# Later turns of q and k, pairs of output blocks, and stored weight pairs in a two-layer encoder kernel

## The chip, the cores and the metric

One Trainium2 chip, one of its cores. The metric is the device time of one execution in microseconds (us), as the median of several runs. The engines are named as the profile names them: PE (TensorE matmul), PEld (its weight load, which overlaps PE), DVE (VectorE), ACT (ScalarE), POOL (GpSimd) and SP (SyncE, which here issues most DMAs; ACT issues a few). A name such as L475 is a line of the kernel before the change.

## The reference

The input x is 2048 tokens by 1024 channels. Two layers run over it:

```
# layer 0: pooling mixer
h = rms_norm(x, a_norm);  u, z = split(h @ w_in)
pooled = trailing means of u over 2, 4, 8, 16 tokens (one window per group of 256 channels) - u
x = x + ((pooled @ w_group) * scale * silu(z)) @ w_out
x = x + (p[0] @ ple_w[0]) * sigmoid(x @ ple_gate_w[0])
# shared keys and values, once
k, v = split(rms_norm(x, kv_norm) @ w_kv);  k = rms_norm per head of 64 (16 heads)
# layer 1: stick-breaking attention
q, z = split(rms_norm(x, b_norm) @ b_w_in);  q = rms_norm per head
a[t, s] = beta[t, s] * product over s < j < t of (1 - beta[t, j]),  beta = sigmoid(q k / 8),  s < t only
x = x + ((a @ v) * silu(z)) @ b_w_out
x = x + (p[1] @ ple_w[1]) * sigmoid(x @ ple_gate_w[1])
```

Everything is float32. The kernel reaches that precision by splitting each operand into a high and a low part (a "pair") and adding three matmuls: high by high, high by low, low by high.

## The kernel before

**Tiles and chunks.** The tokens are cut into four chunks of 512 (`NSUB`, index s or c). Activations are tiles of 128 channels by 512 tokens, kept as pairs. For each chunk `first_part(s)` runs the mixer (`mixer`), its output projection (`out_steps`), the gated embedding (`gate_steps`), the gate z of layer 1 (`gate_z`), and q, k and v of heads 0 to 7 (`kvq(s, kind, 0)`); `second_part(s)` runs q, k and v of heads 8 to 15. `post(c)` is layer 1's projection and embedding (again `out_steps` and `gate_steps`). These generators yield after every matmul and are joined in one stream.

**Attention beside it.** The attention loop at the end of the kernel goes over slots (query chunk c, head h, key chunk kc), 160 of them with four steps each. Step n does `front` (logits by two matmuls L628 and L629, a sigmoid, a scan L635 on DVE), `turn` of the step `LAG_T` = 5 before (four transposes L646, then the pair: ACT copy L649 and DVE subtraction L650, into an `at` tile, two buffers) and `gather` of the step `LAG_G` = 6 before (two matmuls L658 and L659 with v). Between these, `fill` takes matmuls from the stream, at a rate per step that depends on the chunk: 26.8 in the first, 6.2 in the last (`rate`). So the dense work hides attention's chains. `post(3)` runs alone at the end. Everything before the q, k, v of the first chunk's heads 8 to 15 also runs without attention.

**Accumulators.** `dense()` takes PSUM banks: from six when nothing but the stream runs (`solo`), from two, named psd, beside attention. `turned()` takes one of the two psa banks, which the attention turns use too.

**Weights.** `plan` lists all weight units in the order of use: [128 channels, 2 (high and low), 512 values], 512 KB as a pair, 256 KB raw. `unit` loads one on SP (L146), through an `io` buffer (six of them), and splits it on ACT (L135, L129) and on DVE or POOL (L136, L131); if the unit is marked `keep`, the pair is stored to DRAM (L150), and later uses load the pair itself (L143). There are nine buffers for pairs (`UNITS`); `give_back` frees one after its last matmul and `pump` starts the next. In a block of two outputs (`product`) the four units go back one after another during the second output. In `kvq` all eight units of a product stay until its fourth token tile (j = 3) and go back one by one there. Weights of z and of the layer 0 gate z are kept; q, k and v weights (`plan_wide`) are split again in each chunk: 48 units a chunk.

**q and k.** `kvq` makes token-major tiles of 128 tokens by 512 channels, 24 matmuls each (L421). `keyed` scales them (ACT L459), squares them (ACT L461), sums per head (DVE L463), takes the power -1/2 on POOL (L113, L114) and scales the rows (DVE L466). After the fourth tile it appends four closures `finish(m)` to the list `lag`: four transposes on PE (L475), the pair on ACT and DVE (L481 and L482, or L117 and L118), a store (L484). `kvq` of the next kind calls them after matmul groups kt = 2 and kt = 5 of its token tiles j = 0 and j = 1. `valued` shifts v by one token through DMAs on ACT's queue (L437 to L444) and writes the last row of each tile to `ve`; `differences` makes the pair and stores it.

**Other steps that the change touches.** `load_ends` reads `ve` back for the attention of a group of heads, turns it by four tiny transposes (L614) and an ACT copy (L616). `gate_z` computes the norm of its input after its first output and needs the broadcast of it (`token_norm`, `bcast`, L266, L274) to evacuate that output. `fold(g)` multiplies the group map into the u weights at the start (L248); `prep(s)` loads and splits a chunk of x.

**Order.** Each engine works through its own queue in a fixed order, SP's and ACT's DMA issues included. The order is made when the program is built: as written, but a planner with costs of its own may put an instruction that it holds ready ahead of one that waits.

## Time and profile before

| What | us |
|---|---|
| median of 3 runs | 2962.69 |
| lowest and highest | 2959.23, 2965.87 |
| the profiled execution | 2961.81 |
| its span, first to last instruction | 2960.0 |
| PE busy | 2763.0 |
| DVE busy | 1955.7 |
| ACT busy | 1355.7 |
| POOL busy | 966.2 |

The mean clock granted to PE over the span is 0.975. The DMAs moved 588.96 MB, 199 GB/s on average. Busy time of PE is made of modelled ends: matmuls overlap, so a busy PE can still run below its pace, but an idle PE is idle. A row of waits reads: the engine and the tile and line that waited, `<-` what ended the wait, then total us, number of waits, the longest. In a table of stages a row has the stretch, its length, the busy us of PE, PEld, DVE, ACT and POOL with their instruction counts, the granted clock, the DMA share and GB/s. In a list in order of time a row has its start, its length, the engine and line, the operation with out<-in, the count merged, and in brackets the idle time before it.

### The profile page before, as it was taken

Reading aid. Unit: us, or ns where it says so; the run is one execution under the profiler, and the core shown is the slowest. Engines: PE = TensorE matmul, PEld = TensorE weight load, DVE = VectorE, ACT = ScalarE, POOL = GpSimd, SP = SyncE. Lnnn points to the kernel's source line nnn. Section 1 sums busy time; section 2 is a strip of 40 time slices with the busy share of each in tenths; the row PEclk is TensorE's granted clock in tenths of the full one; section 3 lists DMA queues with packets and bytes.
Section 4 is the critical chain, followed back from the end, with each engine's and each line's share of the span. In section 5 each row is a group of like instructions: output and inputs, shape, how many; then the busy total and the mean of one; then the engine's idle time right before and its main releaser. Section 6 shows DMA issues by size and latency. Waiting matters only on the chain. (4 is left out here: it accounts for less than half of the span.)

```text
span 2960.0 us, 39525 instructions
## 1 busy us (share of the span) xinstructions
PE 2763.0 (93%) x13376; PEld 2260.2 (76%) x13376; DVE 1955.7 (66%) x2513; ACT 1355.7 (46%) x2642; POOL 966.2 (33%) x961
## 2 busy tenths in 40 slices
PE   6999898999888999998899999999899999999989
PEld 5878677777776787876777877877678888888767
DVE  6645454655455677756667878776767877778862
ACT  4334453344544344545543455455544444444541
POOL 3454433555533244443222445222211211111111
PEclk9999999999989999999999999999999999999999
DMA  8747468877755755654556445745466777657534
GB/s 282 262 135 252 160 216 293 263 230 260 230 172 185 249 165 153 196 178 144 176 193 213 154 146 153 250 139 163 154 202 206 241 218 226 214 192 228 181 122 164
DMA packets 279062, 588.96 MB, mean 199 GB/s; under 512 B 33830, under 2 KB 66598, under 8 KB 278860
## 3 DMA queue, kind: packets, MB, share of 16 engines
q1 hardware_dynamic: 272096, 577.96, 60.8%
q10 hardware_dynamic: 6764, 8.47, 1.1%
q8 instruction: 107, 1.75, 0.3%
q14 instruction: 95, 0.78, 0.1%
HBM read 442.07 MB, written 135.86 MB: 195 GB/s over the span
## 5 line engine op out<-in xcount | busy, mean ns | idle before, releaser
L635 DVE TENSOR_TENSOR_SCAN pp<-pp,zeros 128x512 f32<-128x512 f32 (+3 forms) x640 | 779.2, 1219 | 119.5 <-POOL pp L633 91.4
L421 PE MATMUL psd<-wpair,x 128*128 128x512 f32 x2304 | 623.9, 408 | 2.2 <-DVE wpair L136 1.4
L649 ACT CAST at<-psa 128x512 fp32r<-128x512 f32 (+3 forms) x640 | 332.8, 520 | 606.0 <-PE psa L646 526.5
L650 DVE TENSOR_TENSOR at<-psa,at 128x512 fp32r<-128x512 f32 (+3 forms) x640 | 384.9, 603 | 320.1 <-ACT at L649 318.2
L421 PEld LDWEIGHTS psd<-wpair,x 128*128 128x128 f32 x2304 | 437.0, 196 | 89.7 <-DVE wpair L136 4.1
L646 PE MATMUL psa<-ident,pp 128*128 128x128 f32 x2176 | 348.9, 275 | 12.9 <-DVE at L650 6.4
L646 PEld LDWEIGHTS psa<-ident,pp 128*128 128x128 f32 x2176 | 278.4, 142 | 94.4 <-DVE pp L635 8.3
L631 ACT ACTIVATE pp<-psl 128x512 f32<-128x512 f32 (+3 forms) x640 | 343.6, 538 | 10.2 <-PE psl L629 7.2
L221 PE MATMUL psd<-x,wpair 128*128 128x512 f32 x768 | 304.7, 397 | 9.7 <-ACT sg L397 6.1
L223 PE MATMUL psd<-x,wpair 128*128 128x512 f32 x768 | 303.7, 395 | 0.2 <-DVE x L118 0.2
L226 PE MATMUL psd<-x,wpair 128*128 128x512 f32 x768 | 302.9, 394 | 0.0
L628 PE MATMUL psl<-kk,qa 128*128 128x512 f32 (+3 forms) x640 | 285.1, 446 | 0.0
L633 POOL TENSOR_SCALAR_AFFINE_SELECT pp<-pp 128x128 f32<-128x128 f32 x256 | 89.5, 350 | 554.4 <-ACT pp L631 553.8
L659 PE MATMUL pso<-at,vv 128*128 128x512 f32 (+3 forms) x640 | 239.9, 375 | 20.8 <-DVE at L650 20.3
L658 PE MATMUL pso<-at,vv 128*128 128x512 f32 (+3 forms) x640 | 233.9, 366 | 5.8 <-ACT at L649 5.7
L629 PE MATMUL psl<-kk,qb 128*128 128x512 f32 (+3 forms) x640 | 236.4, 369 | 0.0
L221 PE MATMUL psd<-xp,wpair 128*128 128x512 f32 x512 | 202.2, 395 | 6.2 <-DMA wpair<-once 3.8
L223 PE MATMUL psd<-xp,wpair 128*128 128x512 f32 x512 | 201.7, 394 | 0.0
L226 PE MATMUL psd<-xp,wpair 128*128 128x512 f32 x512 | 201.5, 393 | 0.0
L136 DVE SCALAR_TENSOR_TENSOR wpair<-wraw,gains,wpair 128x512 fp32r<-128x512 f32 (+1 forms) x224 | 165.9, 782 | 35.0 <-ACT wpair L135 34.5
L221 PEld LDWEIGHTS psd<-x,wpair 128*128 128x128 f32 x768 | 145.7, 190 | 40.4 <-ACT sg L397 7.5
L135 ACT ACTIVATE wpair<-wraw,gains 128x512 fp32r<-128x512 f32 (+1 forms) x224 | 145.7, 688 | 57.4 <-DMA wraw<-in_w_kv_dram 16.9
(134 smaller groups left out, 4664.8 us busy)
## 6 DMA issues: line engine op xcount, KB each, us to landing
wpair<-once SPq DMA_DIRECT2D x240, 512.0 KB
kk<-kd SPq DMA_DIRECT2D x320, 128.0 KB
vv<-vd SPq DMA_DIRECT2D x160, 256.0 KB
wpair<-wf SPq DMA_DIRECT2D x64, 512.0 KB
wraw<-in_w_kv_dram SPq DMA_DIRECT2D x128, 256.0 KB
once<-kp SPq DMA_DIRECT2D x36, 512.0 KB
once<-wpair SPq DMA_DIRECT2D x32, 512.0 KB
wraw<-in_a_w_out_dram SPq DMA_DIRECT2D x64, 256.0 KB
```

The costliest lines, as they stand in the source:

```text
L221: T.matmul(ps, hi, acts[kt][:, 0], start=(i == 0), stop=False)
L223: T.matmul(ps, hi, acts[kt][:, 1], start=False, stop=False)
L226: T.matmul(ps, lo, acts[kt][:, 0], start=False, stop=(i == n))
L421: T.matmul(ps, ck["x2"][kt][:, xh, tk], u[:, wh, 0], start=(kt == 0 and xh == wh), stop=(kt == KT - 1 and wh == 1))
L628: T.matmul(ps[:, :w], qa[:, qs], kk[:, :w], start=True, stop=False)
L629: T.matmul(ps[:, :w], qb[:, qs], kk[:, :w], start=False, stop=True)
L631: A.activation(out=pp[:, r0:], in_=ps[:, :w], func=AF.Sigmoid, scale=-1.0)
L635: V.tensor_tensor_scan(out=pp[:, r0:][:, ::-1], data0=pp[:, r0:][:, ::-1], data1=zeros.to_broadcast([P, w]), initial=1.0 if st["diag"] els ...
L646: T.transpose(pt[:, j * P : (j + 1) * P], pp[:, r0 + kt * P : r0 + (kt + 1) * P], ident)
L649: A.copy(out=at[:, 0, cs], in_=pt[:, cs])
L650: V.tensor_tensor(out=at[:, 1, cs], in0=pt[:, cs], in1=f(at[:, 0, cs]), op=ALU.subtract)
L659: T.matmul(po[:, cs], vv[:, kt, :], at[:, 1, cs], start=False, stop=(st["last"] and kt == 3))
```

## The change

Eight edits:

- `LAG_G` goes from 6 to 7, the `at` tile gets a third buffer, an `io` buffer is taken away (five), and a slot's v is loaded at its neighbour's step 3 instead of 2.
- The four `finish` calls move from (j, kt) = (0, 2), (0, 5), (1, 2), (1, 5) to (1, 2), (1, 5), (2, 1), (2, 4). `vs` moves from the `row` buffers, which hold q's or k's rows longer now, to `tmp`.
- `product2` takes the first two outputs of `out_steps`, `gate_steps` and `gate_z` together: the first three units for both outputs, then the last unit for both; all units go back at its end.
- `gate_z` copies its first two outputs out of PSUM unscaled, computes the norm after them, and puts the broadcast into the next block.
- q, k, v weights are kept: the first chunk stores the pairs, the others load them.
- `load_ends` reads the ends by four DMAs on ACT's queue, in transposed order, 4 bytes an element, with no transposes.
- At the start `fold` requests the u tiles (on SP) before it takes the group map's weights; these weights and half of the first chunk's x are requested on ACT's queue, and only two weight units may be out until half of the first chunk of x is split.
- The first chunk's x is loaded ahead (`load_first`) into q, k, v and pp buffers.

```
-LAG_T, LAG_G = 5, 6
+LAG_T, LAG_G = 5, 7
-    io = flat("io", 6)
+    io = flat("io", 5)
-    att = ... tag="at", name=nm, bufs=2)
+    att = ... tag="at", name=nm, bufs=3)
...
-        nc.sync.dma_start(out=raw, in_=src[:, kts[0] : kts[-1] + 1])
+        wq["by"].dma_start(out=raw, in_=src[:, kts[0] : kts[-1] + 1])
...
-        while wq["out"] < len(plan) and wq["out"] - wq["back"] < UNITS:
+        while wq["out"] < len(plan) and wq["out"] - wq["back"] < wq["cap"]:
...
-            plan.append(((nm, b, kt), src[b], (kt,), W5, gain, False))
+            plan.append(((nm, b, kt), src[b], (kt,), W5, gain, True))
...
+    def product2(pss, us, acts):
+        n = sum(len(kts) for _, kts in us)
+        i = [0, 0]
+        for part, back in ((us[:-1], False), (us[-1:], True)):
+            for k in range(2):
+                for u, kts in part:
+                    for e, kt in enumerate(kts):
+                        hi, lo = (u[:, l, e, k * P : k * P + P] for l in range(2))
+                        T.matmul(pss[k], hi, acts[kt][:, 0], start=(i[k] == 0), stop=False)
+                        yield
+                        T.matmul(pss[k], hi, acts[kt][:, 1], start=False, stop=False)
+                        yield
+                        i[k] += 1
+                        T.matmul(pss[k], lo, acts[kt][:, 0], start=False, stop=(i[k] == n))
+                        yield
+        for _ in us:
+            give_back()
...
+    def load_first():
+        for o in range(KT):
+            xin = (qryt, ppt, keyt, valt)[(0, 2, 0, 3, 0, 2, 0, 3)[o]]("xin", F32)
+            (nc.sync, nc.scalar)[o % 2].dma_start(out=xin, in_=x[o * P : (o + 1) * P, 0:W5])
+            first_x.append(xin)
...
@@ out_steps, gate_steps
+            pss = [dense(), dense()] if b == 0 else []
+            if pss:
+                yield from product2(pss, us, acts)
...
-                if kt in (2, 5) and j < 2 and lag:
+                if lag and (j, kt) in ((1, 2), (1, 5), (2, 1), (2, 4)):
                     lag.pop(0)()
...
-        vs = row("vs")
+        vs = tmp("vs")
...
@@ gate_z
+        yield from product2(pss, us, ck["x2"])
+        for k in range(2):
+            zr = row("zr")
+            A.copy(out=zr, in_=pss[k])
+            first.append(zr)
+        ck["r2"] = token_norm(ck["acc2"], "y")
...
+                for i, _ in enumerate(product(ps, us, ck["x2"], k * P, k)):
+                    if o == 2 and i == 20:
+                        ck["rb2"] = rb = bcast(ck["r2"], "y")
...
@@ load_ends
-        for m in range(4):
-            T.transpose(pt[:, 0, 4 * m : 4 * m + 4], raw[0:4, m * P : (m + 1) * P], ident[0:4, 0:4])
+        for j in range(4):
+            nc.scalar.dma_start(out=en[:, :, j], in_=ve[c][b][j].rearrange("(m q) -> q m", q=P))
...
+    start = fold(3)
+    next(start)
+    load_first()
...
-            if j == 2 and i + 1 < len(slots):
+            if j == 3 and i + 1 < len(slots):
                 begin_v(i + 1)
```

More of the change, by code (lines that the diff above doesn't have):

```diff
@@ L123, in trunk_kernel @@
     plan = []
-    wq = {"out": 0, "taken": 0, "back": 0}
+    wq = {"out": 0, "back": 0, "cap": 2, "by": nc.scalar}
     held = deque()
@@ L295, in prep @@
         for o in range(KT):
[L296 to L297 removed]
+            if s:
+                xin = io("xin")
+                nc.sync.dma_start(out=xin, in_=x[o * P : (o + 1) * P, s * W5 : (s + 1) * W5])
+            else:
+                xin = first_x[o]
             pr = pair("xp")
@@ L368, in out_steps @@
                 nc.sync.dma_start(out=xr, in_=residual(2 * b + k))
-                ps = dense()
-                yield from product(ps, us, acts, k * P, k)
+                if pss:
+                    ps = pss[k]
+                else:
+                    ps = dense()
+                    yield from product(ps, us, acts, k * P, k)
                 V.tensor_tensor(out=xr, in0=ps, in1=xr, op=ALU.add)
@@ L389, in gate_steps @@
             us, ul = take(4), take(1)
+            pss = [dense(), dense()] if b == 0 else []
+            if pss:
+                yield from product2(pss, us, x1)
             for k in range(2):
@@ L393, in gate_steps @@
                 G.tensor_tensor(out=xj, in0=f(x1[o][:, 0]), in1=f(x1[o][:, 1]), op=ALU.add)
-                ps = dense()
-                yield from product(ps, us, x1, k * P, k)
+                if pss:
+                    ps = pss[k]
+                else:
+                    ps = dense()
+                    yield from product(ps, us, x1, k * P, k)
                 sg = tmp("sg")
@@ L511, in gate_z, with put @@
         ck = chunk[s]
-        for b in range(4):
+        def put(o, zr):
+            sg = tmp("sg")
+            A.activation(out=sg, in_=zr, func=AF.Sigmoid)
+            G.tensor_tensor(out=zr, in0=zr, in1=sg, op=ALU.mult)
+            nc.sync.dma_start(out=zd[s][o], in_=zr)
+        us = take(4)
+        pss = [dense(), dense()]
+        yield from product2(pss, us, ck["x2"])
+        first = []
+        for k in range(2):
[3 more added lines that the diff above has]
+        ck["r2"] = token_norm(ck["acc2"], "y")
+        for b in range(1, 4):
             us = take(4)
@@ L713, in trunk_kernel @@
                            op0=ALU.mult, op1=ALU.mult)
-    for _ in fold(3):
+    wq["by"] = nc.sync
+    for _ in start:
         pass
     side = prep(0)
-    for _ in range(KT):
+    for _ in range(4):
         next(side)
-    for _ in fold(2):
+    wq["cap"] = UNITS
+    second = fold(2)
+    next(second)
+    for _ in range(4):
+        next(side)
+    for _ in second:
         pass
```

40 lines of the change are left out of this document (20 added, 20 removed).

## The prediction

> **What bounds the kernel now.** I read the page's head, then the waits of TensorE (PE), then a table of stages, then the instructions around one wait.
>
> ```profile
> span 2960.0 us, 39525 instructions
> PE 2763.0 (93%) x13376; PEld 2260.2 (76%) x13376; DVE 1955.7 (66%) x2513; ACT 1355.7 (46%) x2642; POOL 966.2 (33%) x961
> ```
>
> PE is busy 93% of the span and nothing else comes near it, so a gain must come out of PE's 197 us of idle time (2960.0 - 2763.0) or out of time at half clock. Who ends PE's waits, in us in total, times, longest:
>
> ```profile
> PE pst L475 <- DVE qs L466: 70.8, 16, 9.7
> PE psd L248 <- ACT uh L239: 24.4, 4, 19.3
> PE pso L659 <- DVE at L650: 20.3, 29, 2.7
> PE psd L221 <- ACT mp L117: 9.8, 4, 4.7
> ...
> PE psd L221 <- DVE zr L312: 6.0, 3, 3.6
> ...
> PE pso L658 <- ACT at L649: 5.7, 6, 2.4
> ...
> PE psd L223 <- POOL mp L118: 4.7, 5, 1.7
> PE pst L266 <- POOL r L114: 4.0, 4, 1.5
> ...
> PE pst L614 <- DMA ends<-ve: 3.7, 2, 2.9
> ```
>
> By line, with the idle time before each group behind the bar:
>
> ```profile
> L475 PE MATMUL pst<-ident,qs 128*128 128x128 f32 x256 | 47.1, 300 | 83.5 <-DVE qs L466 70.8 <-DVE at L650 5.9 <-ACT op L117 5.4
> ```
>
> The turns of q and k (L475) own 83.5 us of idle time. The matmuls of q, k and v:
>
> ```profile
> L421 PE MATMUL psd<-wpair,x 128*128 128x512 f32 x2304 | 623.9, 408 | 2.2 <-DVE wpair L136 1.4 <-ACT wpair L135 0.6
> ```
>
> They wait 2.2 us in all: weights are never late today. By stage (start, the four q, k, v stages, the end of attention), with the granted clock, the DMA share and GB/s in the last columns; the last row is a stretch in which the DMAs are full:
>
> ```profile
> 0.00:41.00 41.00, 17.68 (x104) 17.05 (x105) 24.62 (x74) 22.20 (x44) 14.61 (x17) 0.92 0.80 277
> 295.00:474.00 179.00, 155.48 (x701) 126.09 (x700) 80.87 (x116) 81.29 (x140) 64.64 (x65) 0.94 0.61 198
> 778.00:981.00 203.00, 175.97 (x833) 143.19 (x832) 108.50 (x154) 98.85 (x189) 77.23 (x79) 0.93 0.59 185
> 1318.00:1552.00 234.00, 207.72 (x1000) 168.74 (x999) 149.57 (x200) 122.32 (x235) 69.11 (x81) 0.95 0.54 171
> 1946.00:2206.00 260.00, 235.47 (x1163) 190.41 (x1162) 181.76 (x240) 137.44 (x260) 61.16 (x70) 0.96 0.50 158
> 2776.00:2862.00 86.00, 73.09 (x386) 54.13 (x385) 79.73 (x97) 52.60 (x104) 5.70 (x11) 1.00 0.30 91
> 720.00:740.00 20.00, 19.16 (x98) 15.90 (x97) 7.07 (x12) 5.39 (x11) 6.23 (x7) 1.00 1.00 352
> ```
>
> PE loses about 25 us of idle time in each q, k, v stage, and only there does the clock sit at 0.93 to 0.96 for long. From 2776 DVE is busy 79.73 of 86 us: that end is DVE's and the change doesn't touch it.
>
> **The turns.** One wait, on ACT and then on PE:
>
> ```profile
> 319.18 0.67 ACT L459 ACTIVATE qs<-psd,r 128x512 f32<-128x512 f32 x1
> 319.71 0.99 SPq L297 DMA_DIRECT2D xin<-in_x_dram  x2
> ...
> 324.19 0.62 ACT L117 CAST xp<-xin 128x512 fp32r<-128x512 f32 x1 [1.62 <-DMA xin<-in_x_dram]
> ...
> 325.25 0.61 ACT L461 ACTIVATE sqq<-qs 128x512 f32<-128x512 f32 x1
> ...
> 331.48 0.66 PE L475 MATMUL pst<-ident,qs 128*128 128x128 f32 x2 [7.49 <-DVE qs L466]
> ...
> 338.74 14.56 PE L421 MATMUL psd<-wpair,x 128*128 128x512 f32 x63
> ```
>
> The squares (L461) stand on ACT behind an x tile that waits for its DMA, so the normalised rows come 12 us after the copy of L459. The change moves all four turns 24 matmuls later; each is four transposes, an ACT copy, a DVE subtraction and a store on SP's queue. At 14.56/63 = 0.231 us a matmul that is 5.5 us without attention; in the second stage, attention in between, (203 - 27)/576 = 0.306, so 7.3 us. The longest wait, 9.7, keeps 2.4, nearly all others nothing. Stages two to four hold 83.5 less the first stage's 21.4:
>
> ```profile
> DVE qs L466: 21.4, 4
> ```
>
> 62 us, of which I take 60. The moved stores delay only q and k loads of attention, which come later still. Lost clock there is at most 0.07 x 203 + 0.05 x 234 + 0.04 x 260 = 36 us; part of it falls on idle time, and I take 20 (bounds 0 and 36).
>
> **Weights as pairs.** From the second chunk on, 144 units lose one ACT and one DVE operation and load 512 KB instead of 256:
>
> ```profile
> L136 DVE SCALAR_TENSOR_TENSOR wpair<-wraw,gains,wpair 128x512 fp32r<-128x512 f32 (+1 forms) x224 | 165.9, 782 | 35.0 <-ACT wpair L135 34.5
> ```
>
> That is 144 x 0.78 = 113 us of DVE, and the same number of ACT copies, none on PE's path (L421 waits 1.4 + 0.6 us for splits): worth nothing by itself. What it costs: a product of q, k or v holds eight of nine pair buffers until its fourth tile. Today the next raw tiles already wait in the io buffers and only have to be split; a stored pair can't be asked for until its buffer is free. So seven loads of 0.524 MB go out in a burst on SP, and the last is needed 42 matmuls after the first buffer comes free. At 352 GB/s seven take 10.4 us; the x tile above (0.262 MB, 0.7 us of transfer) landed 4.5 us after its issue, so 3.7 us more: 14.1. PE needs it after 42 x 0.306 = 12.8 us in the second stage, 15.2 in the third (234 - 26 over 576), 17.2 in the fourth. Lower bound: 1.3 us at each of five transitions in the second stage, 6.5 in all. Upper bound: the stages' other traffic (185 less 62 GB/s of raw weights, and so on: 123, 117, 110) goes on in the burst, seven loads then take 16.0, 15.6 and 15.2 us, and the waits are 6.9, 4.1 and 1.7 us, five each: 63 us. I take 27, nearer the lower end, because stores of turned tiles now fall into tiles two and three, not into the burst. What hid this was partly the wait on the turns itself.
>
> In the first chunk 48 stores of 0.524 MB (25.2 MB) are added on SP, each behind its split. The DMAs are busy 0.61 x 179 = 109 us there; with 25.2 MB at 352 GB/s, 72 more: 181 us, while PE without its waits and lost clock (21.4 and 0.06 x 179) needs 147. The DMAs bind. Bounds: +2 and -32; prefetch and trailing stores stretch the DMAs' window somewhat: I take -8.
>
> **Attention a step later.** L659 and L658 wait 20.3 + 5.7 us; in the end from 2776 they are DVE's, there
>
> ```profile
> PE pso L659 <- DVE at L650: 10.4, 15, 1.3
> ```
>
> of them. The rest, 15.6, has waits up to 2.7 us; a step of the last chunk holds 6.2 dense matmuls (by rate) and four of attention's, 10 x 0.231 = 2.4 us, earlier ones more: -13 (bounds 0 and -16). The third at buffer carries it; the v load moves one step back too and keeps its distance.
>
> **First blocks of two.** The last pair of inputs is needed after 36 matmuls instead of 18, 4.2 us more, against waits of up to 4.7 (mp): -13 of 9.8 + 4.7. The norm's turn (L266, 4.0) and the bank that the first silu holds (the 3.6 of zr) go under the next block: -8. New: after such a block both banks are full and the third product has six matmuls, 1.4 us, of cover for a DVE or ACT evacuation that can stand behind a scan of 1.2 us:
>
> ```profile
> L635 DVE TENSOR_TENSOR_SCAN pp<-pp,zeros 128x512 f32<-128x512 f32 (+3 forms) x640 | 779.2, 1219 | 119.5 <-POOL pp L633 91.4 <-ACT pp L631 25.1
> ```
>
> With 0.7 us for the evacuation itself (L459's 0.67 above, also out of PSUM), 1.2 + 0.7 - 1.4 = 0.5 us in 15 places with two banks (three stages of three chunks, two of three posts): +7. Bounds: 0, and 1.9 each without the cover, 28.
>
> **Ends.** PE's 3.7 us go: -3. Four DMAs move to ACT's queue, where they wait for the store of the same ends and hold sigmoids and copies behind them; one hold is bounded by 3.7 us of latency and four issues of 0.5 (0.99 for two above), 5.7 us, times 8 = 46 us if all of it reached PE. Attention's lag of five and seven steps covers it: 0.
>
> The Trainium skill (DMA: Bandwidth & Descriptors, Rules for kernel authors) says that a non-contiguous last dimension becomes one descriptor an element, which speaks against these loads of 4 bytes each; no run here shows one, and by it I would go some way to the upper end.
>
> **Start.** PE's first matmul came 7.1 us after the u loads were issued:
>
> ```profile
> 12.22 4.02 SPq L237 DMA_DIRECT2D uraw<-in_wu_t_dram  x4
> 19.28 0.80 PE L248 MATMUL psd<-wpair,uh 128*128 128x256 f32 x2 [19.28 <-ACT uh L239]
> ```
>
> Issued first, it comes at about 8, 11 us earlier. But the first 41 us move the same bytes at share 0.80, which is 33 us of full DMA: at most 8. I take -7.
>
> **Sum.** -60 - 20 + 27 - 8 - 13 - 21 + 7 - 3 - 7 = -98. The profiled execution took 2961.8 us (span 2960.0), so 2864; its median, 2962.7, is 0.9 higher: 2865.
>
> **Rivals.** *Weights come in time*: 6.5 instead of 27 and -32 instead of -8 in the first chunk: 2820. For it: DMA share only 0.50 to 0.59. The same Trainium skill page (Bandwidth; the fit stands under Anatomy of one DMA) has 2.0 us + bytes/436 GB/s for a DMA; an estimate by it for the seven loads is 10.4 us, no wait anywhere. No run here shows that. *The turns still wait*: with fuller DMAs the x tile in ACT's way lands later; if half of the 60 and of the 20 stay, and 10 more are lost around them: 2915. Against it: the cover is now 9 + 24 matmuls, 7.6 to 10.1 us, and only chains as long as the one shown exceed it. *Slower*: the seven loads get too little. Without the 27 the gains are 125 us over 20 transitions (the first chunk's too), so it decides from 6.3 us a transition: 3.7 + 3.67 MB/r - 15 = 6.3, r = 208 GB/s. At 190 GB/s each waits 8 us, 160 in all: 2998. Against it: other traffic takes 110 to 123 GB/s, which leaves 229. *It doesn't do what it says*: the turns stay where they were in PE's order: 2865 + 80 = 2945.
>
> **Chances.** Forecast 0.45, weights in time 0.25, turns still wait 0.17, slower 0.06, no move 0.05, all cancels 0.02. This kernel's measurement tells 0.2% from nothing. Faster 0.92, same 0.02, slower 0.06. The range, 2805 to 2930, holds the forecast with its bounds, the first rival and most of the second.
>
> **What would show it.** Right: L475's wait below 15 us, clock above 0.97 in the stages from 778, L421 with tens of us behind wpair<-once DMAs at each product's first tile, DMA share near 0.9 from 295 to 474, first matmul near 8 us. Wrong: L421 still at 2 us; L475 above 40; ACT waits for ends that PE feels.

## The result, and the profile after

The changed kernel takes 2936.47 us (median of five runs, 2930.39 to 2947.1) against 2962.97 us before (five runs). The ratio is 0.9909 (95% interval 0.9884 to 0.9935): 26 us faster, where 98 were forecast. 2936.47 lies above the upper end of the range, 2930, so the sign was right and the size was not.

The head of the changed kernel's page; the lines answer to those of the page before:

```profile
span 2934.7 us, 38858 instructions
PE 2755.9 (94%) x13344; PEld 2254.8 (77%) x13344; DVE 1859.2 (63%) x2369; ACT 1269.8 (43%) x2498; POOL 956.0 (33%) x961
DMA packets 302802, 651.84 MB, mean 222 GB/s; under 512 B 51462, under 2 KB 84230, under 8 KB 302604
```

DVE and ACT lost some 90 us of work each, as the pairs were to bring, and the DMAs move 63 MB more (588.96 before). PE's idle time only fell from 197 to 179 us. Who ends PE's waits now (us in total, times, longest). Lines have moved: the turns of q and k are L521 (L475 before), the matmuls of q, k, v L467 (L421), attention's turn L708 (L646) and its product L720 and L721 (L658, L659):

```profile
PE psa L708 <- DVE at L712: 23.4, 31, 3.0
PE pst L521 <- DVE qs L512: 16.7, 6, 4.7
PE psa L708 <- DVE pp L697: 16.2, 20, 2.6
PE psd L467 <- ACT wpair L135: 13.4, 7, 4.9
PE psd L467 <- DMA wpair<-once: 12.1, 10, 3.0
PE pst L521 <- DVE hl L528: 11.7, 8, 3.3
```

The groups by line, the idle time before them behind the bar:

```profile
L467 PE MATMUL psd<-wpair,x 128*128 128x512 f32 x2304 | 622.5, 407 | 37.0 <-ACT wpair L135 13.4 <-DMA wpair<-once 12.1 <-DVE zr L587 9.0
L708 PE MATMUL psa<-ident,pp 128*128 128x128 f32 x2176 | 351.6, 276 | 47.3 <-DVE at L712 23.4 <-DVE pp L697 16.2 <-DVE hl L528 2.4
...
L721 PE MATMUL pso<-at,vv 128*128 128x512 f32 (+3 forms) x640 | 235.7, 368 | 0.0
L720 PE MATMUL pso<-at,vv 128*128 128x512 f32 (+3 forms) x640 | 232.9, 364 | 0.1
...
L521 PE MATMUL pst<-ident,qs 128*128 128x128 f32 x256 | 42.4, 285 | 29.0 <-DVE qs L512 16.7 <-DVE hl L528 11.7 <-ACT ss L299 0.3
```

In the kernel before, attention's turn stood so:

```profile
L646 PE MATMUL psa<-ident,pp 128*128 128x128 f32 x2176 | 348.9, 275 | 12.9 <-DVE at L650 6.4 <-DVE pp L635 4.9 <-DVE hl L482 1.3
```

Two things stand out. Attention's product waits for nothing any more, but the turn before it went from 12.9 to 47.3: a wait has moved by one place. And the matmuls of q, k and v, never late before (2.2 us), now wait 37.0. By stage (stretch, length, busy us of PE, PEld, DVE, ACT and POOL, clock, DMA share, GB/s); the first two rows are q, k, v of the first chunk, heads 0 to 7 and 8 to 15, then the mixer of the second chunk, then q, k, v of the second, third and fourth chunk:

```profile
291.00:374.00 83.00, 73.37 (x312) 56.95 (x310) 32.75 (x42) 35.08 (x57) 37.21 (x32) 0.96 0.77 266
374.00:489.00 115.00, 92.97 (x384) 71.90 (x383) 53.01 (x73) 46.48 (x82) 33.75 (x39) 0.90 0.84 287
489.00:615.00 126.00, 110.53 (x489) 89.05 (x487) 64.27 (x89) 36.41 (x76) 48.78 (x54) 0.93 0.81 261
817.00:1013.00 196.00, 170.98 (x801) 138.97 (x800) 79.85 (x110) 73.22 (x146) 75.26 (x83) 0.95 0.78 257
1340.00:1555.00 215.00, 203.71 (x1001) 165.36 (x1000) 117.89 (x157) 94.98 (x186) 66.42 (x78) 0.98 0.71 236
1947.00:2184.00 237.00, 226.10 (x1157) 185.97 (x1156) 152.64 (x196) 112.30 (x218) 55.89 (x68) 0.99 0.66 216
```

The third and fourth chunk gained (215 us against 234, 237 against 260). The first lost: heads 8 to 15 take 115 us at a clock of 0.90, and the mixer behind them 126. The same two stretches of the kernel before:

```profile
383.00:474.00 91.00, 81.11 (x370) 65.61 (x369) 46.74 (x68) 44.25 (x79) 29.98 (x33) 0.94 0.72 233
474.00:580.00 106.00, 102.07 (x480) 83.82 (x478) 61.04 (x85) 33.83 (x74) 47.26 (x57) 1.00 0.88 291
```

So the first chunk with its stores is where the gain went first. The list in order of time shows one of its holes, in the changed kernel:

```profile
390.79 2.25 SPq L150 DMA_DIRECT2D once<-wpair  x2
...
393.24 2.52 SPq L146 DMA_DIRECT2D wraw<-in_b_w_q_dram  x2
...
399.44 2.07 ACT L135 ACTIVATE wpair<-wraw,gains 128x512 fp32r<-128x512 f32 x3 [2.75 <-DMA wraw<-in_b_w_q_dram]
...
400.21 9.93 PE L467 MATMUL psd<-wpair,x 128*128 128x512 f32 x35 [4.87 <-ACT wpair L135]
```

SP issues two stores of pairs, then the raw loads; ACT waits for such a load, splits it at 399.44, and PE has stood 4.87 us when it goes on at 400.21.

A measure used below: for each pair of neighbouring matmuls in a trace, the time between their starts beyond the matmul's own pace at full clock, added up by stage. This "lost" time of PE holds idle time and the time lost at a lower clock together.

### The profile page after: what moved, and what is told of

Read it like the earlier page. It is cut to its first block, busy times and chain, and to the rows that moved or that the text cites. A ratio compares the mean times of both kernels' runs of the same rounds, so it can differ in the third digit from the quotient of the medians.

```text
span 2934.7 us, 38858 instructions
## 1 busy us (share of the span) xinstructions
PE 2755.9 (94%) x13344; PEld 2254.8 (77%) x13344; DVE 1859.2 (63%) x2369; ACT 1269.8 (43%) x2498; POOL 956.0 (33%) x961
## 5 line engine op out<-in xcount | busy, mean ns | idle before, releaser
L467 PE MATMUL psd<-wpair,x 128*128 128x512 f32 x2304 | 622.5, 407 | 37.0 <-ACT wpair L135 13.4
L711 ACT CAST at<-psa 128x512 fp32r<-128x512 f32 (+3 forms) x640 | 332.7, 520 | 618.9 <-PE psa L708 568.1
L712 DVE TENSOR_TENSOR at<-psa,at 128x512 fp32r<-128x512 f32 (+3 forms) x640 | 383.6, 601 | 286.2 <-ACT at L711 283.7
L467 PEld LDWEIGHTS psd<-wpair,x 128*128 128x128 f32 x2304 | 435.9, 195 | 136.3 <-DMA wpair<-once 18.6
L708 PE MATMUL psa<-ident,pp 128*128 128x128 f32 x2176 | 351.6, 276 | 47.3 <-DVE at L712 23.4
L708 PEld LDWEIGHTS psa<-ident,pp 128*128 128x128 f32 x2176 | 273.6, 142 | 140.6 <-DVE at L712 29.1
L721 PE MATMUL pso<-at,vv 128*128 128x512 f32 (+3 forms) x640 | 235.7, 368 | 0.0
L720 PE MATMUL pso<-at,vv 128*128 128x512 f32 (+3 forms) x640 | 232.9, 364 | 0.1
L221 PE MATMUL psd<-x,wpair 128*128 128x512 f32 x576 | 227.0, 394 | 0.0
L223 PE MATMUL psd<-x,wpair 128*128 128x512 f32 x576 | 226.0, 392 | 0.0
L226 PE MATMUL psd<-x,wpair 128*128 128x512 f32 x576 | 225.4, 391 | 0.0
L221 PE MATMUL psd<-xp,wpair 128*128 128x512 f32 x512 | 205.3, 402 | 18.0 <-DMA wpair<-wf 5.4
L223 PE MATMUL psd<-xp,wpair 128*128 128x512 f32 x512 | 203.2, 397 | 0.0
L226 PE MATMUL psd<-xp,wpair 128*128 128x512 f32 x512 | 203.1, 397 | 0.0
L131 POOL TENSOR_TENSOR wpair<-wraw,wpair 128x512 fp32r<-128x512 f32 x98 | 144.5, 1481 | 73.7 <-ACT wpair L129 73.3
L721 PEld LDWEIGHTS pso<-at,vv 128*128 128x128 f32 x640 | 122.3, 191 | 25.5 <-DVE at L712 0.2
L720 PEld LDWEIGHTS pso<-at,vv 128*128 128x128 f32 x640 | 122.0, 191 | 25.6 <-ACT at L711 0.4
```

Of the source, the lines that this page charges most:

```text
L221: T.matmul(ps, hi, acts[kt][:, 0], start=(i == 0), stop=False)
L223: T.matmul(ps, hi, acts[kt][:, 1], start=False, stop=False)
L226: T.matmul(ps, lo, acts[kt][:, 0], start=False, stop=(i == n))
L467: T.matmul(ps, ck["x2"][kt][:, xh, tk], u[:, wh, 0], start=(kt == 0 and xh == wh), stop=(kt == KT - 1 and wh == 1))
L708: T.transpose(pt[:, j * P : (j + 1) * P], pp[:, r0 + kt * P : r0 + (kt + 1) * P], ident)
L711: A.copy(out=at[:, 0, cs], in_=pt[:, cs])
```

## The experiments

Every run is compared with the kernel before on the same chip. All times are medians. The kernel before took 2960.6 to 2963.5 us beside the several runs, so a difference of 3 us between two runs of different chips can be that of the chips.

### The pairs

**No pairs.** One part of the changed kernel undone:

```
-            plan.append(((nm, b, kt), src[b], (kt,), W5, gain, True))
+            plan.append(((nm, b, kt), src[b], (kt,), W5, gain, False))
```

> The changed kernel with one part undone: the q, k, v weights are not stored as pairs; every chunk loads them raw and splits them, as the kernel before does. Counting the time that TensorE loses in each stage (time between two matmul starts beyond the matmul's own), the changed kernel loses 22.0 us more than the kernel before in heads 8 to 15 of chunk 0's q, k, v stage (38.8 against 16.8), 19.5 us more in the first stage of chunk 1 (26.2 against 6.7), and 19.7 and 22.4 us less in the q, k, v stages of chunks 2 and 3. Theory A (the stores and pair loads cost the 41 us early, and the later turns bring the 42 us late): the early loss goes, the late gain stays, 2895 us (2885 to 2910). Theory B (the early loss is the pairs', but the late gain too is theirs, because ScalarE and VectorE no longer split): both go, 2935 us (2925 to 2950). Theory C (the early loss is not the pairs', it comes from five general buffers in place of six and the new attention lag, and the late gain is the turns'): 2936 us with the early loss still in its place.

Measured: 2907.86 us, ratio 0.9816 (0.9798 to 0.9835). The pairs cost 28.6 us (2936.5 - 2907.9). Theory A holds within its range; B and C, which leave the time at 2935 or 2936, don't.

**Stores alone.** Chunk 0 stores, later chunks load raw:

```
-        if key in once:
+        if key in once and keep != "store":
```

> The changed kernel, in which chunk 0 still stores the q, k, v weights as pairs (25.2 MB written), but chunks 1 to 3 load them raw and split them again. It tells the price of the stores from that of the pair loads. Theory A1 (the stores are the early price: the raw loads behind them on the in-order queue come late): chunk 0's 22.0 us of added loss stay, and the time is that of the changed kernel within 10 us, 2930 us (2920 to 2945). Theory A2 (it is the pair loads, twice the bytes in the later chunks, that cost): about 2910 us or less. Theory B (the late gain of 42 us comes from pair loads): 2975 us (2960 to 2990).

Measured: 2957.0 us, ratio 0.9977 (0.9967 to 0.9987). The stores cost 49.1 us (2957.0 - 2907.9) and the pair loads bring 20.6 back (2957.0 - 2936.5). None of the theories had put these two together: the loads, for which the forecast charged 27, are a gain.

**The same bytes from a tile that is long ready.**

```
-            nc.sync.dma_start(out=once[key], in_=f(pr))
+            stored = chunk[0]["x2"][kts[0]] if keep == "store" else pr
+            nc.sync.dma_start(out=once[key], in_=f(stored))
```

> As the run in which chunk 0 only stores the q, k, v pairs and the later chunks load raw (2957 us, 49 us above the run without pairs), but each of these stores writes a tile that has long been ready (a normed activation of chunk 0, the same 512 KB) in place of the pair just split. What is stored is read by nothing, so the output is the reference's. The bytes and the number of stores stay, the wait of each store for the second half of its split goes. Theory A (the stores hold the transfer queue's issuing engine, which works in order: each waits for VectorE's half of the split, and the next raw loads are issued only behind it): most of the 49 us go, 2925 us (2910 to 2935). Theory B (the 25.2 MB themselves crowd the transfers, whose share of busy time is 0.84 to 0.91 there): the time stays at 2957 us (2945 to 2965).

Measured: 2940.44 us, ratio 0.9925 (0.991 to 0.9941). 16.6 of the 49.1 go, 32.6 stay: between the theories. This run takes two things from the store: the wait for its split, and the hold on the pair's buffer, which can't be filled again before the store has read it. The next two runs were to part them.

**Stores three units later**, in the changed kernel:

```
+        while pend and (len(pend) > 2 or not keep):
+            d, q = pend.popleft()
+            nc.sync.dma_start(out=d, in_=f(q))
```

> The changed kernel, every store of a pair is issued three units later, behind the raw loads of the next units, so that it finds its split finished; bytes, stores and pair loads stay. Theory A (the in-order wait of the stores is what costs): 2936 - 25 to 45, so 2900 us (2890 to 2915). Theory B (the bytes cost): 2936 us (2925 to 2945).

Measured: 2942.89 us, ratio 0.9939 (0.9925 to 0.9953): no gain, but no clean answer, since the edit also delays the stores of z's pairs and the first output stage begins 7 us later (154.8 against 147.5, starts of matmuls in the traces). So the same was done for q, k and v only, with raw loads in the later chunks:

> As the run in which chunk 0 only stores the q, k, v pairs (2957 us) while later chunks load raw, but each q, k, v store is issued three units later, so that its split is long done; bytes and queue stay, and the pair's buffer is held longer. With a ready tile in place of the pair it took 2940 us. Theory A (the 17 us between them are the stores' wait for the split, which holds the issuing order): 2940 us (2934 to 2946). Theory B (they are the pair's buffer, taken until its store has landed): 2957 us or more (2950 to 2965).

Measured: 2956.37 us, ratio 0.9979 (0.9969 to 0.9989), the 2957.0 of the stores alone. From 291 to 490 us of the traces, SP's stores of pairs wait 35.0 us for their splits in the run with the stores alone and 14.8 in this one, and nothing is gained. Either that wait costs nothing, or the buffer, which a later store holds longer, takes back what the shorter wait gives. That the 17 us are the pair's buffer, held until its store has landed, is argued and not shown: no run gives more buffers.

**Half the bytes**, 48 stores of 256 KB:

```
+            part = slice(0, 1 if keep == "store" else 2)
+            nc.sync.dma_start(out=once[key][:, part], in_=f(stored)[:, part])
```

> As the run in which chunk 0 stores a ready tile in place of each q, k, v pair (2940 us, 32 us above the run without pairs), but only the first half of each tile is stored: the same 48 stores of 256 KB instead of 512 KB, 12.6 MB instead of 25.2. Theory A (the bytes crowd the transfers): half of 32 us goes, 2924 us (2918 to 2930). Theory B (it is the number of stores, each taking a place in the issuing order): 2940 us (2935 to 2945). Theory C (half the bytes fit into the gaps that the transfers have): 2910 us.

Measured: 2909.13 us, ratio 0.9818 (0.9805 to 0.9831). The 12.6 MB cost 1.3 us (2909.1 - 2907.9), the 25.2 MB 32.6. There are 48 stores in both, so it isn't their number that has the price, and the cost doesn't go with the bytes either. It looks as if only what exceeds some room in the queue had a price; where that room ends, two amounts don't tell.

**The other queue.** The full 25.2 MB of ready tiles, issued by ACT:

```
+            (nc.scalar if keep == "store" else nc.sync).dma_start(out=once[key], in_=f(stored))
```

> As the run in which chunk 0 stores a ready tile in place of each q, k, v pair (2940 us), but the 48 stores are issued by ScalarE into its own transfer queue, which carries 10 MB in all against 601 MB on SyncE's. Bytes and number of stores stay. Theory A (loads stand behind the stores in the one queue): with the stores out of it most of the 32 us go, 2912 us (2908 to 2920). Theory B (the 16 transfer engines' time is what is short, whatever the queue): 2940 us (2932 to 2946).

Measured: 2916.74 us, ratio 0.9844 (0.983 to 0.9857). 23.7 of the 32.6 us go. Its stages, q, k and v of heads 0 to 7 and 8 to 15 and the mixer of the second chunk:

```profile
299.00:386.00 87.00, 76.57 (x333) 61.21 (x332) 38.64 (x53) 41.02 (x68) 38.83 (x35) 0.94 0.84 292
386.00:473.00 87.00, 78.41 (x361) 62.80 (x360) 43.94 (x65) 40.36 (x72) 29.93 (x33) 0.98 0.82 259
473.00:582.00 109.00, 102.19 (x480) 83.69 (x478) 60.37 (x87) 35.21 (x75) 48.83 (x56) 1.00 0.87 291
```

The DMAs are as busy as in the changed kernel (0.84, 0.82, 0.87), and 87 and 109 us replace 115 and 126. So the DMA engines' time was not what ran short. This run and the one with the same tiles on SP's queue differ in the queue alone; there the loads stand behind the stores. The Trainium skill (DMA: Bandwidth & Descriptors, section on queues, rings and completion order) says that SP and ACT each own a row of rings, consumed in ring order, between which the DMA engines take turns; the two runs, 2940 and 2917 us, agree with it, though no trace here looks into the rings.

PE's lost time by stage, in us, worked out from the traces:

| q, k, v unless named | before | after | no pairs | stores alone | ready tile | ACT's queue |
|---|---|---|---|---|---|---|
| chunk 0, heads 8-15 | 16.8 | 38.8 | 12.5 | 39.3 | 21.1 | 13.8 |
| chunk 1, mixer | 6.7 | 26.2 | 7.3 | 22.8 | 18.8 | 9.4 |
| chunk 1, first output | 17.5 | 23.8 | 11.8 | 23.2 | 23.6 | 11.3 |
| chunk 1, all heads | 42.1 | 39.0 | 41.3 | 41.4 | 38.8 | 39.0 |
| chunk 2, all heads | 46.1 | 26.4 | 29.7 | 28.6 | 27.6 | 29.5 |
| chunk 3, all heads | 45.6 | 23.2 | 36.0 | 35.9 | 35.9 | 37.0 |

The chunks are counted from 0, as in the code. The pair loads show in the last row above all: 23.2 against 36 in all the shown runs with raw loads and the later turns; so a part of theory B of the first run is true.

### The turns, the blocks, the lag, the ends

**The turns alone**, in the kernel before:

```
-                if kt in (2, 5) and j < 2 and lag:
+                if lag and (j, kt) in ((1, 2), (1, 5), (2, 1), (2, 4)):
-        vs = row("vs")
+        vs = tmp("vs")
```

> The kernel before with one part of the change alone: the four turns of q, k are finished a tile later, and the shifted values live in the short-lived buffers so that the rows stay free. The turns waited 83.5 us in the kernel before and 28 us in the changed one. Theory A (later turns are worth nearly what they waited, and are what made chunks 2 and 3 shorter): 2963 - 45 to 60, so 2910 us (2900 to 2920). Theory B (most of what the turns no longer wait for is waited for elsewhere, and the gain in chunks 2 and 3 is the pair loads'): 2950 us (2940 to 2963).

Measured: 2907.23 us, ratio 0.9814 (0.9797 to 0.9831), 56.3 us faster. By line:

```profile
L659 PE MATMUL pso<-at,vv 128*128 128x512 f32 (+3 forms) x640 | 239.5, 374 | 28.8 <-DVE at L650 28.0
L475 PE MATMUL pst<-ident,qs 128*128 128x128 f32 x256 | 42.5, 285 | 37.8 <-DVE qs L466 22.8 <-DVE hl L482 10.7 <-DVE at L650 2.2
```

The turns go from 83.5 to 37.8, not to nearly nothing: eight waits for rows are left, and 10.7 us are a new wait of one turn for the copy out of the bank that the turn before it used. L659, attention's product, waits 28.0 us for DVE, where it waited 20.3 before. One edit gives twice what all eight give together.

**The first blocks alone**, in the kernel before: the new `product2`, its use in `out_steps` and `gate_steps`, and the new `gate_z`.

> The kernel before with one part alone: the first two output blocks of each product of the four small stages are taken together, the norm of the gate's first blocks is put behind them, and the product waits no more for it. My forecast gave this 13 + 8 us saved and 7 us of new waits. Theory A (that sum): 2963 - 14, so 2949 us (2940 to 2955). Theory B (the turns alone gave 56 us and everything but the pairs gave 56 too, so the blocks, the start, the lag and the ends give nothing in sum: the blocks give about 10 us, and lag and start take it back): 2953 us (2948 to 2958). Theory C (the blocks give nothing because their waits only move): 2963 us (2958 to 2968).

Measured: 2939.08 us, ratio 0.9927 (0.991 to 0.9943), 23.5 us faster, more than any of the three theories. PE's idle time falls from 197.0 to 184.6 us (span less busy time). The waits for mp (9.8 and 4.7) and at L266 (4.0) are gone, and a new one of 6.3 us is there: the paired blocks wait for DVE, which still empties a bank, before they start and not behind them, where the forecast had put its 7. The clock goes from 0.975 to 0.977.

**Both and nothing else:**

> The kernel before with two parts and no others: the later turns (alone 56 us faster) and the first two blocks together with the gate's norm behind them (alone 23 us faster). It keeps the old start, the attention lag of six with six general buffers, raw q, k, v weights and the old loading of the ends. Theory A (the two add up, and the new start and ends of the changed kernel bring nothing): 2963 - 56 - 23 = 2884 us (2876 to 2890), no slower than the run without pairs at lag six (2888). Theory B (start and ends are worth the 10 us of my forecast): 2898 us. Theory C (the two overlap, since both shorten the q, k, v stages' surroundings): 2900 us or more.

Measured: 2887.42 us, ratio 0.9744 (0.9731 to 0.9757). The blocks bring 19.8 on top of the turns, so the two nearly add up.

**Lag six** beside the pairs, with two `at` buffers and six `io` buffers:

```
-LAG_T, LAG_G = 5, 7
+LAG_T, LAG_G = 5, 6
-    io = flat("io", 5)
+    io = flat("io", 6)
-    ... tag="at", name=nm, bufs=3)
+    ... tag="at", name=nm, bufs=2)
-            if j == 3 and i + 1 < len(slots):
+            if j == 2 and i + 1 < len(slots):
```

> The changed kernel with the attention lag back at six (LAG_G 6, two buffers for the turned weights in place of three, six general buffers in place of five, values loaded one row of work earlier). In the kernel before, the two matmuls that use the turned weights waited 26.6 us in all and the turns 12.9; in the changed kernel 0.1 and 47.3. Theory: the wait only moved from the use to the turn, so the lag brings nothing, and this kernel takes 2936 us (2930 to 2942). Rival 1 (the lag is worth the 13 us of my forecast): 2949 us. Rival 2 (five general buffers hold back the raw weight loads of chunk 0 and are part of the early loss): 2915 us.

Measured: 2929.05 us, ratio 0.9892 (0.9875 to 0.9909), some 7 us below the changed kernel, with intervals that overlap. The same without the pairs:

> The changed kernel without the q, k, v pairs (2908 us) and with the attention lag back at six, two buffers of turned weights, six general buffers. The lag at six beside the pairs was 7 us faster than the changed kernel. Theory A (lag seven is worth nothing anywhere, and five general buffers cost): 2901 us (2895 to 2907). Theory B (six general buffers helped only because raw loads and stores stood in each other's way): 2908 to 2916 us, the weight-folding at the start, which shares the two buffers, losing 9 us as it did there.

Measured: 2888.46 us, ratio 0.9751 (0.9735 to 0.9767): 19.4 us below the run without pairs. The lag, with what paid for it, is a loss. The pairs cost 40.6 us at lag six (2929.1 - 2888.5) and 28.6 at lag seven, so the prices of the parts don't simply add up. Three runs take the lag apart. Five general buffers:

> The run without pairs at lag six (2888 us, six general buffers), with five general buffers instead of six and nothing else changed. Lag seven with its third buffer of turned weights and five general buffers took 2908 us. Theory A (the general buffer that lag seven was paid with is what costs the 20 us): 2908 us (2902 to 2912). Theory B (the lag itself costs, because values are loaded later and the turn now waits behind the previous tile's copies): 2888 us (2884 to 2894).

Measured: 2893.96 us, ratio 0.9764 (0.9749 to 0.9779). The buffer may be worth 5.5 us; the intervals overlap. The values loaded later:

> The run without pairs at lag six with five general buffers (2894 us), in which the values of the next tile are loaded one row of work later, as lag seven has it, and nothing else is changed. Theory A (the lag itself costs the 14 us: the turn now waits where the product waited, at the head of the row of work): 2894 us (2889 to 2899). Theory B (the later loads cost): 2908 us (2902 to 2912).

Measured: 2896.43 us, ratio 0.9781 (0.9763 to 0.9798), 2.5 us, not told from nothing. Only the lag (and the values) set back in the run without pairs, three `at` and five `io` buffers kept:

> The changed kernel without pairs (2908 us) with only the lag set back from seven to six and the values' load with it; three buffers of turned weights and five general buffers stay. Theory A (the lag itself costs what is left of the 20 us, and the third buffer saves up to 9 us at the start): 2889 us (2884 to 2894). Theory B (the third buffer, not the lag, is what costs): 2905 us or more.

Measured: 2890.24 us, ratio 0.9765 (0.9741 to 0.9789): lag seven itself costs 17.6 us (2907.86 - 2890.24). The groups at lag six in this run:

```profile
L708 PE MATMUL psa<-ident,pp 128*128 128x128 f32 x2176 | 346.8, 273 | 11.8 <-DVE pp L697 5.0 <-DVE at L712 2.8 <-DVE hl L528 2.1
...
L721 PE MATMUL pso<-at,vv 128*128 128x512 f32 (+3 forms) x640 | 238.5, 373 | 27.4 <-DVE at L712 26.8
L720 PE MATMUL pso<-at,vv 128*128 128x512 f32 (+3 forms) x640 | 232.2, 363 | 7.2 <-ACT at L711 7.1
```

and at lag seven, in the run without pairs, with its turns of q and k:

```profile
L708 PE MATMUL psa<-ident,pp 128*128 128x128 f32 x2176 | 350.6, 275 | 46.1 <-DVE at L712 24.1 <-DVE pp L697 12.4 <-DVE hl L528 4.4
...
L721 PE MATMUL pso<-at,vv 128*128 128x512 f32 (+3 forms) x640 | 234.9, 367 | 0.0
L720 PE MATMUL pso<-at,vv 128*128 128x512 f32 (+3 forms) x640 | 231.5, 362 | 0.0
...
L521 PE MATMUL pst<-ident,qs 128*128 128x128 f32 x256 | 43.7, 291 | 47.8 <-DVE qs L512 26.0 <-DVE hl L528 14.4 <-DVE at L712 5.1
```

11.8 + 27.4 + 7.2 = 46.4 against 46.1: not one microsecond of waiting is saved. PE gets past the product sooner and stands at the next turn, for the most part (24.1 us) because the turn's bank still has to be read by the copies L711 and L712. What differs most is the clock: 0.983, 0.985, 0.985 and 0.986 in the four executions at lag six, 0.977, 0.980, 0.981 and 0.981 in the four at lag seven. By the middle of each, (1 - 0.985) x 2890 = 43 us and (1 - 0.9805) x 2908 = 57 us are lost, 13 of the 17.6 us. PE's idle time differs by 5.5 us in the traces (160.5 and 166.0).

The Trainium skill (TensorE: Matmul & The Clock Gate, Part 1) says that the clock is halved after an idle window of some 3.4 us. The traces show the half clock after shorter waits too. In the trace at lag seven, PE goes on at 1684.02 us after one wait of 2.57 us at L708, and the next 3.4 us run at half clock (0.50, the third column from the end in the second row):

```profile
1684.02 0.48 PE L708 MATMUL psa<-ident,pp 128*128 128x128 f32 x1 [2.57 <-DVE pp L697]
```

```profile
1684.00:1687.40 3.40, 3.38 (x10) 2.80 (x11) 2.94 (x3) 2.83 (x7) 3.40 (x3) 0.50 0.58 225
```

So that single wait costs some 1.7 us more, half of 3.4. But it isn't shown that the moved waits are the ones that cost the clock. The two traces, at 0.983 and 0.977, are 18 us of lost clock apart. Some 11 of them, 0.05 x 215, fall between 570 and 785 us, in the small stages of the second chunk (clock 0.97 at lag six, 0.92 at lag seven), and there PE's waits are those of dense products; attention's turns wait 1.1 us in that stretch at lag seven. Why lag seven loses more clock stays open.

**The ends** loaded by ACT's DMAs, added to turns and blocks:

```
-        for m in range(4):
-            T.transpose(pt[:, 0, 4 * m : 4 * m + 4], raw[0:4, m * P : (m + 1) * P], ident[0:4, 0:4])
+        for j in range(4):
+            nc.scalar.dma_start(out=en[:, :, j], in_=ve[c][b][j].rearrange("(m q) -> q m", q=P))
```

> The kernel with the later turns and the first blocks alone (2887 us), with the ends loaded by four DMAs on ScalarE's queue in place of the tiny transposes, and nothing else. Theory A (the new ends are what the run with new start, new ends and lag six makes up its 8 us with): 2879 us (2874 to 2884). Theory B (the ends are worth the 3 us of the forecast or nothing, and the new start's order of loads is what helps later): 2886 us (2884 to 2890).

Measured: 2882.91 us, ratio 0.9735 (0.9713 to 0.9757), 4.5 us below the run without it, with overlapping intervals. It has the lowest median of this study, 54 us below the changed kernel.

### Pairs in the faster kernel

Half of the pairs, `kt % 2 == 0` in place of `True` in `plan_wide`, added to turns and blocks:

> The kernel with the later turns and the first blocks alone (2887 us), in which every second row block of the q, k, v weights is stored as pairs by chunk 0 and loaded as pairs by chunks 1 to 3: 12.6 MB of stores instead of 25.2. Theory A (stores of half the bytes cost about nothing, and half of the 21 us that pair loads bring is had): 2878 us (2872 to 2884). Theory B (a store also holds its pair's buffer, and pairs keep crowding the later chunks): 2890 us or more.

Measured: 2896.45 us, ratio 0.9778 (0.9761 to 0.9795): 9 us slower than without. These are as many bytes as the 12.6 MB that cost 1.3 us above, but stored from the pairs themselves, and with half of the pair loads; which of the two makes the difference no run tells. All pairs, stored late by ACT:

> The kernel with the later turns and the first blocks alone (2887 us), with all q, k, v pairs stored, by ScalarE's queue and three units late, so that ScalarE does not wait for the split. Theory A (stores outside the loads' queue cost 9 us, pair loads bring 21): 2875 us (2868 to 2884). Theory B (the held buffers cost 17 us more): 2892 us (2886 to 2900).

Measured: 2887.62 us, ratio 0.9748 (0.9727 to 0.9769): between the theories, equal to the kernel without pairs. The rows of q, k, v and of the turns show what is traded. Turns and blocks alone:

```profile
L452 PE MATMUL psd<-wpair,x 128*128 128x512 f32 x2304 | 612.9, 403 | 2.0 <-DVE wpair L136 2.0
...
L506 PE MATMUL pst<-ident,qs 128*128 128x128 f32 x256 | 43.2, 288 | 34.8 <-DVE qs L497 21.2 <-DVE hl L513 8.9 <-DVE at L701 2.4
```

and with all pairs through ACT's queue:

```profile
L462 PE MATMUL psd<-wpair,x 128*128 128x512 f32 x2304 | 617.8, 404 | 40.4 <-DMA wpair<-once 21.0 <-ACT qs L500 10.2 <-DVE wpair L137 7.3
...
L516 PE MATMUL pst<-ident,qs 128*128 128x128 f32 x256 | 41.3, 280 | 14.1 <-DVE hl L523 7.5 <-DVE qs L507 5.1 <-ACT ss L305 0.9
```

With less work on DVE and ACT the turns wait less, 34.8 to 14.1; the matmuls of q, k and v wait more, 2.0 to 40.4. Attention's turn and product make up most of the rest: they wait 53.2 us without and 38.1 with the pairs, so that PE's idle time is 144 and 145 us.

## Why the prediction was right or wrong

The runs form a chain from the kernel before to the changed one: turns 2907.2, blocks 2887.4, ends 2882.9, new start with three `at` and five `io` buffers 2890.2, lag seven 2907.9, pairs 2936.5. The prices hold for this order; in another order they differ (the blocks alone 23.5, the pairs at lag six 40.6). The forecast's terms beside its steps (the forecast put 32 us of the turns' gain, waits and clock of the first stage, into its term for the first chunk; 32 - 8 = 24 is what it charged the stores):

| Part | forecast | measured |
|---|---|---|
| turns, with lost clock | -60 - 20 - 32 = -112 | -56.3 |
| first blocks, norm, two banks | -21 + 7 = -14 | -19.8 |
| ends | -3 | -4.5 |
| start (measured with the buffers) | -7 | +7.3 |
| lag seven | -13 | +17.6 |
| pairs: loads | +27 | -20.6 |
| pairs: stores | +24 | +49.1 |
| sum | -98 | -27 |

Of the 71 us by which the forecast missed, the turns make 56, the lag 31 and the start 14; the pairs cost 22 less than forecast and the blocks gave 6 more. That the pairs as a whole (28.6 against 51) come near is luck: the loads missed by 48 us one way and the stores by 25 the other.

- **The turns** failed in size, and it was their waits. "The longest wait, 9.7, keeps 2.4, nearly all others nothing": in the run with the turns alone, 37.8 of 83.5 us stayed, among them eight waits for rows, the longest 5.5. The step measured the cover against the rows' delay and left out that the later turns come close to each other and share a bank (10.7 us); and attention's product waits longer (28.0 instead of 20.3 at L659). Over the whole kernel PE's idle time fell by 35 us (197 to 162), where the step had counted 60 + 21. The clock did come back as forecast: from 0.975 to 0.984 over the span, 27 us, where 20 + 11 were counted. The reading that the clock is low for long "only there" was not right, though: in the small stages of the second chunk, from 580 to 778 us, it was 0.94 too, with 21 us of idle time.
- **The lag** failed in sign. "The third at buffer carries it" was true and beside the point: the next turn needs a free PSUM bank, and the wait moved there whole (46.4 and 46.1). The bound "0 and -16" excluded a loss without a reason. Why it is a loss of 17.6 and not nothing stays open; the clock was lower in each execution.
- **The pair loads** failed in sign. PE's waits for pair loads are 12.1 us, near the lower bound of 6.5; but splitting less was not "worth nothing by itself". With the stores in both, the turns, whose chain runs over ACT and DVE, wait 44.7 us with raw loads and 29.0 with pair loads, and attention's turns 58.1 and 47.3; the matmuls of q, k and v wait 20.5 and 37.0.
- **The stores** were undersized by half. "The DMAs bind" named the wrong limit: shares of 0.77 and 0.84 were reached, not full engines, and ACT's queue carried the same bytes for 8.9 us in place of 32.6. The queue that the loads share bound, and perhaps the held buffers (17 us, argued only), and the price ran on into the mixer of the second chunk, which the step left out.
- **The blocks** were right in sign and undersized, -14 against -19.8 to -23.5. The waits came out nearly as summed: idle time fell by 12.4 us in the run with the blocks alone. Some 6 us of the rest are clock, (1 - 0.975) x 2960 = 74 us against (1 - 0.977) x 2938.5 = 68, which the term didn't hold.
- **The start.** The first matmul came at 11.4 us, not at 8 (before: 19.3), and the first output stage began at 147.5 instead of 144.5: 8 us gained, 11 lost in the mixer behind. The kernel at lag six without pairs, with the new start and ends, ties with the one that has neither (2888 and 2887). It differs from the kernel with turns, blocks and ends in the start alone: 2888.5 against 2882.9, 5.6 us slower, with overlapping intervals. So a gain of 7 is not to be seen, and a loss isn't shown.
- **The ends** fit the forecast, though 4.5 us is not told from nothing. For loads of 4 bytes an element the page's head shows, without and with them:

```profile
DMA packets 279062, 588.96 MB, mean 204 GB/s; under 512 B 33830, under 2 KB 66598, under 8 KB 278860
```

```profile
DMA packets 295893, 588.95 MB, mean 205 GB/s; under 512 B 50694, under 2 KB 83462, under 8 KB 295692
```

  16,864 packets more under 512 B, for eight loads of 4 x 512 elements, 16,384 in all: the Trainium skill's rule (DMA: Bandwidth & Descriptors, Rules for kernel authors), one descriptor an element, holds in the count, nearly. No cost in time can be seen here.
- **What would show it**: L521 at 29.0 us lies between the two marks of 15 and 40; the clock is 0.95, 0.98 and 0.99 instead of above 0.97 throughout; the weights wait, but a third of it for pair loads; the DMA share is below 0.9.
- **The rivals**: "it doesn't do what it says" came nearest in time (2945), but by chance: the turns did move, and alone they gave 56 us. "The turns still wait" (2915) named a part of what happened. "Weights in time" was near for the loads (12.1 us, with 6.5 named) and wrong for the stores. "Slower" named the loads at the transitions, which gained. The first rival quotes 2.0 us + bytes/436 GB/s; the Trainium skill (DMA: Bandwidth & Descriptors, Anatomy of one DMA) gives this fit for DMAs issued by GpSimd, while these loads were issued by SP, and "no wait anywhere" did not come true.

## What to carry to other kernels

An edit that only lets an engine pass one wait sooner can be worth nothing, or cost, as long as the next resource on the way (here the PSUM bank of the next turn) is not free as well; follow the wait to where it goes before it is booked as a gain. Bytes added to the queue that also carries urgent loads are to be costed by what stands behind them in that queue, not by the DMA engines' share alone. And an operation off the critical path (the splits on DVE and ACT) can still be in the way of one that is on it. A set of edits wants a run for each part: two of these eight, alone, beat all eight by 49 us.

## What was not expected of the hardware

- The granted clock is part of a wait's price: a single wait of 2.57 us was followed by 3.4 us at half clock. And a sum of waits doesn't tell the clock: with 46 us of them at attention's turn and product in both, the clock was 0.983 to 0.986 at lag six and 0.977 to 0.981 at lag seven.
- The price of stores doesn't go with their bytes: 12.6 MB of tiles long ready, added to SP's queue in the first chunk, cost 1 us (2909.1 against 2907.9), 25.2 MB cost 33, and the same 25.2 MB on ACT's queue cost 9.
